# The low part of each weight: a subtraction on GpSimd and VectorE replaced by a negated copy on ScalarE and an accumulating DMA

## The chip, the cores and the metric

The kernel runs on one core of one Trainium2 chip. The metric is the device time of one execution in microseconds. A core has five engines with instruction queues of their own, which the profile calls PE (TensorE, matrix products; its weight loads are listed apart as PEld), DVE (VectorE), ACT (ScalarE), POOL (GpSimd) and SP (SyncE, which here only issues DMAs). DMAs run on 16 DMA engines that all queues share.

## The reference

The reference is one inference step of two trunk layers over 1024 prompt tokens and 64 sample tokens, all in float32:

```
h = rms_norm(x) * (1 + scale) + shift
u, v, z_a, q, k, val, z_b, g_a, g_b = split(h @ w_in)          # w_in: 1024 x 10240
y_a = gelu(u) * spatial_mix(layer_norm(gelu(v))) * silu(z_a)
y_b = combine(3 dilated window attentions of q, k, val) * silu(z_b)
merged = sigmoid(g_a) * (y_a @ w_gm_out) + sigmoid(g_b) * (y_b @ w_att_out)
x = x + gate * (merged @ w_o)
```

Outputs are the normalised result, the new keys and values, and the rows of the spatial mixer for the samples. The four weight matrices w_in, w_gm_out, w_att_out and w_o are what the change is about.

## The kernel before

**Three products in place of one.** TensorE multiplies float32r, a form of float32 with a shortened mantissa. To keep float32 precision, each operand is held as a high part (its float32r copy) and a low part (the operand minus the high part). A product of activations and weights is three matmuls: high by high, high by low, low by high. The activations are split once and stay; the weights come from HBM as raw float32 and are split on the way.

**A weight tile.** The unit is 128 x 1024 float32 (512 KB). `w_load` has SP issue the DMA of the raw tile (`wraw`); `w_split` makes `whi` with an ACT copy and `wlo` with `tensor_tensor(subtract)`, through the helper `split`, which takes the engine as `eng`: POOL on the whole tile, or for `"both"` POOL on the left half and DVE on the right half. `w_get` hands over the next tile. All raw, high and low tiles, and many others, rotate through one pool of 20 slots, so a new tile can wait for the last reader of an old one. 280 weight tiles are used, 140 for each layer.

**Main loop.** 80 of a layer's tiles are jobs on w_in. For each job `piece` runs three pieces of tokens (384, 384 and 320 columns), 24 matmuls each; between the matmuls stand those of attention and of other background work. After the matmuls of piece 0 it calls `w_ahead`, which splits the next job's tile (on POOL) and loads the one after it. The first three jobs of a layer run together, piece by piece.

**Tail.** `tail` runs nine stages for each layer (`stage_b`, `stage_a`, `stage_o`, for each of the three pieces). A weight tile serves only 24 matmuls there, so 60 tiles go by fast. After each tile's matmuls `w_ahead("both", 2)` splits up to two tiles ahead and loads a third. The last call of layer 0 already splits the first two tiles of layer 1.

**Order.** Each engine works through its instructions in the order in which the code is written; the framework adds the semaphore waits. On TensorE the first low part of a weight tile stands third among its matmuls, so a late `wlo` stops TensorE at once, and everything behind it.

Of the kernel before, what the change touches and what calls it, by code (L numbers as in the profile page):

```python
# [24 lines left out]
FT = mybir.dt.float32  # L25
FR = mybir.dt.float32r
AF = mybir.ActivationFunctionType
OP = mybir.AluOpType
# [19 lines left out]
RATE = 3.0  # L48
# [116 lines left out]
JOBS = _job_list()  # L165
# [14 lines left out]
class Builder:  # L180
# [113 lines left out]
    def w_split(self, i, eng=None):  # L294
        if i in self.wraw and i not in self.whl:
            hi = self.slot([128, 1024], FR, "whi")
            lo = self.slot([128, 1024], FR, "wlo")
            self.split(hi, lo, self.wraw.pop(i), eng or self.nc.gpsimd)
            self.whl[i] = (hi, lo)

    def w_get(self, eng=None):
# [431 lines left out]
    def piece(self, l, job, p, hi, lo, state, rate, ahead):  # L733
        nc = self.nc
        ps = self.ps("pj")
        w = PW[p]
        h = self.h[p]
        n = 0
        for k in range(8):
            for a, b in ((hi, 0), (hi, 1), (lo, 0)):  # L740
                nc.tensor.matmul(ps[:, :w], a[:, k, :], h[:, b, k, :w], start=(n == 0), stop=(n == 23))  # L741
                n += 1
            if k in (2, 5):
                self.tick(k // 3, rate)
        if ahead:
            self.w_ahead(ahead)
        self.run_later()
        getattr(self, "ev_" + job[0])(l, job, p, ps[:, :w], state)
        self.tick(2, rate)
# [641 lines left out]
    def tail(self, l, yb):  # L1391
# [31 lines left out]
        def gate_load(p, c, i, gt):  # L1423
            if c < 8:
                n = min(3, 8 - c)
                t = self.slot([128, 3, 384], name="gt")
                self.load(t[:, :n, :PW[p]], self.gs_d[l][p][:, c:c + n, i, :])
                for j in range(n):
                    gt[c + j] = t[:, j, :PW[p]]

        def stage_b(p):
            w = PW[p]
            tmp[p] = self.triple(8, name="tmp")
            gt = {}
            gate_load(p, 0, 1, gt)
            gate_load(p, 3, 1, gt)
            for i in range(4):
                ws = [t.rearrange("p (c k n) -> p c k n", c=2, n=128) for t in self.w_get()]
                for j in range(2):
                    c = 2 * i + j  # L1440
                    ps = self.ps("pj")
                    self.products(ps, w, [t[:, j] for t in ws], yb[p], 4)
                    if j == 0:
                        self.w_ahead("both", 2)
                    step()
                    nc.vector.scalar_tensor_tensor(tmp[p][c][:, :w], gt.pop(c), 1.0, ps[:, :w],
                                                   op0=OP.add, op1=OP.mult)
                    if c == 2:
                        gate_load(p, 6, 1, gt)
            del yb[p]  # L1450

        def stage_a(p):
            w = PW[p]
            m = self.act()
            mg[p] = [[m[:, e, k, :] for k in range(8)] for e in range(2)]
            gt = {}
            gate_load(p, 0, 0, gt)
            gate_load(p, 3, 0, gt)
            for c in range(8):
                ws = [t.rearrange("p (k n) -> p k n", n=128) for t in self.w_get()]  # L1460
                ps = self.ps("pj")
                self.products(ps, w, ws, ya[p], 8)
                self.w_ahead("both", 2)
                step()
                if c:
                    last()
                x = self.half(name="mx")[:, :w]
                nc.vector.scalar_tensor_tensor(x, gt.pop(c), 1.0, ps[:, :w], op0=OP.add, op1=OP.mult)
                nc.vector.tensor_tensor(x, x, tmp[p][c][:, :w], op=OP.add)
                if c == 2:  # L1470
                    gate_load(p, 6, 0, gt)
                last = lambda c=c, x=x: self.split(mg[p][0][c][:, :w], mg[p][1][c][:, :w], x)
            last()
            del ya[p], tmp[p]

        def stage_o(p):
            w = PW[p]
            wp = w if p < 2 else 256
            gate = self.mods[l]["gate"]
            x = self.triple(8, name="x")  # L1480
            self.move_x(x, self.a["xT"][:, :, P0[p]:P0[p] + w] if l == 0 else self.x_d[p], p)
            acc = self.half(name="acc")
            for c in range(8):
                ws = [t.rearrange("p (k n) -> p k n", n=128) for t in self.w_get()]
                ps = self.ps("pj")
                self.products(ps, w, ws, mg[p], 8)
                self.w_ahead("both", 2)
                step()
                if c:
                    self.sumsq(x[c - 1], c - 1, acc, p)  # L1490
                nc.vector.scalar_tensor_tensor(x[c][:, :wp], ps[:, :wp], gate[:, c, 0:1], x[c][:, :wp],
                                               op0=OP.mult, op1=OP.add)
                if wp < w:
                    t = self.half(name="xs")[:, 0:SMP]
                    nc.vector.tensor_tensor(t.rearrange("p (b t) -> p b t", t=NT),
                                            ps[:, wp:w].rearrange("p (b t) -> p b t", t=NT),
                                            gate[:, c, 1:9].unsqueeze(2).to_broadcast([128, NB, NT]), op=OP.mult)
                    nc.vector.tensor_tensor(x[c][:, wp:w], x[c][:, wp:w], t, op=OP.add)
            self.sumsq(x[7], 7, acc, p)
            del mg[p]  # L1500

            if l + 1 < L:
                self.after(lambda: self.move_x(x, self.x_d[p], p, True), 3)

            def finish():
                r = self.rstd(acc, p)
                if p < 2:
                    yield
                    yield
                    yield  # L1510
                rbc = self.rstd_bc(r, p)
                if l + 1 < L:
                    newh[p] = self.act_h(p)
                    yield from self.make_h(l + 1, p, x, rbc, newh[p])
                    return
                for c in range(8):
                    nc.vector.scalar_tensor_tensor(x[c][:, :w], x[c][:, :w], self.ng[:, L, c:c + 1], rbc[:, :w],
                                                   op0=OP.mult, op1=OP.mult)
                    self.store(a["oy"][:, c, P0[p]:P0[p] + w], x[c][:, :w])
                    yield  # L1520
            if p < 2:
                start(("h", p), finish())
            else:
                self.hgen = [iter(()), iter(()), finish()]
            if p == 2:
                if l + 1 < L:
                    self.w_load(self.wi + 3)
                    for i in range(3):
                        self.w_split(self.wi + i, "both")
# [29 lines left out]
    def run(self):  # L1559
# [5 lines left out]
        for l in range(L):  # L1565
# [11 lines left out]
            ws = [self.w_job("both") for _ in range(3)]  # L1577
            states = [{} for _ in range(3)]
            for p in range(NP):
                for _ in self.hgen[p]:  # L1580
                    pass
                for i in range(3):
                    for g in self.hgen[p + 1:p + 2]:
                        for _ in range(6):
                            next(g, None)
                    self.piece(l, JOBS[i], p, *ws[i], states[i], 0, "both" if p == 1 and i == 1 else None)
                    if p == 0 and i == 1:
                        self.w_load(self.wi + 1)
            del ws, states
            for i, job in enumerate(JOBS):  # L1590
                if i < 3:
                    continue
                if l == 0 and i == 3:
                    self.group_select()
                if job == ("ga", 1):
                    self.bgq.append(self.sample(l))
                    if l == 0:
                        self.bgq.append(self.ada(0, (4, 5)))
                    if l + 1 < L:
                        self.bgq.append(self.ada(l + 1, range(6)))  # L1600
                w, st = self.w_job(), {}
                for p in range(NP):
                    self.piece(l, job, p, *w, st, RATE / 3, self.nc.gpsimd if p == 0 else None)
                del w
                if i >= len(JOBS) - 2:
                    for _ in range(4):
                        next(pre, None)
# [102 lines left out]
```

## Time and profile before

| What | Value |
|---|---|
| median of 3 runs | 3130.92 us (3122.43 to 3131.36) |
| the profiled execution | 3131.33 us, its span 3129.5 us |
| TensorE busy | 3010.8 us, 96% of the span |
| DVE, ACT, POOL busy | 54%, 39%, 43% |
| share of the 16 DMA engines taken by the data queue | 45.4% |
| granted TensorE clock over the span | 0.98 |

The span is the time between the first and the last instruction; the other 1.8 us of the execution lie around it. Busy shares are averages over stages of different kinds: in the main loop of each layer (about 60 to 1330 us and 1620 to 2870 us) attention runs beside the projections, in the two tails (about 1370 to 1620 us and 2870 to 3129 us) little but matmuls and weight splitting is left.

### The profile page before, as it was taken

To read this page: it belongs to the slowest core of one execution; us is meant where nothing else is said; L and a number is where in the kernel's file an instruction comes from. 1 tells how busy PE (TensorE), PEld (TensorE's weight loads), DVE (VectorE), ACT (ScalarE), POOL (GpSimd) and SP (SyncE) were. 2 spreads that over 40 slices of the span, in tenths; PEclk is the share of its full clock that TensorE was granted. 3 is DMA by queue.
4 is the path that set the end of the run, shared out by engine and by line. 5 is a ranking of instruction groups with operands and counts; after the bars stand their busy time and mean duration, and the time that the engine had idled before them with its cause. 6 is when DMAs were issued, how large, how long until landed. Compare 5 with 4: busy or idle time off the path is not lost.

```text
span 3129.5 us, 51144 instructions
## 1 busy us (share of the span) xinstructions
PE 3010.8 (96%) x19136; PEld 2865.4 (92%) x19136; DVE 1687.0 (54%) x3583; ACT 1231.3 (39%) x3089; POOL 1357.9 (43%) x959
## 2 busy tenths in 40 slices
PE   6999999999998999999999999999999999999998
PEld 4999899999988998879989999999999889989998
DVE  7445546462265756466773545454513657553666
ACT  5454444444233133343444444444432331322432
POOL 4666556462143322123446755656612432222333
PEclk8999999999999999999999999999999999999999
DMA  6335353444353335466644364435343542434665
GB/s 223 113 103 119 98 101 120 95 121 84 112 180 113 122 108 167 157 236 227 211 153 134 86 142 81 119 106 114 106 81 119 171 130 95 138 102 149 223 211 172
DMA packets 262288, 425.92 MB, mean 136 GB/s; under 512 B 116140, under 2 KB 169144, under 8 KB 262040
## 3 DMA queue, kind: packets, MB, share of 16 engines
q1 hardware_dynamic: 262040, 422.65, 45.4%
q8 instruction: 151, 2.47, 0.3%
q14 instruction: 97, 0.79, 0.1%
HBM read 349.96 MB, written 72.61 MB: 135 GB/s over the span
## 4 chain that ended last, share of the span: by engine, by line
PE 82%; DVE 8%; DMA 4%; issue 3%; ACT 2%; POOL 1%; SPq 0%; DVEq 0%; ACTq 0%; POOLq 0%
PE pspj L741 53%; PE pspj L1382 14%; PE pss L870 4%; PE pso L916 3%; PE pspt L895 2%; PE psmi L602 1%; DMA kq<-in_kc_dram 1%; DVE qb L1218 1%; DMA craw<-in_wada_dram 1%; DVE chl L249 1%; PE psmi L998 1%; DMA wraw<-in_win_dram 1%; ACT whi L243 1%; PE pss L1236 1%; PE pspt L1132 1%
## 5 line engine op out<-in xcount | busy, mean ns | idle before, releaser
L741 PE MATMUL pspj<-act,whi 128*128 128x384 f32 (+1 forms) x7680 | 1967.0, 339 | 6.5 <-DVE act L674 3.5
L741 PEld LDWEIGHTS pspj<-act,whi 128*128 128x128 f32 x7680 | 1352.7, 190 | 42.4 <-issue 7.4
L741 PE MATMUL pspj<-act,wlo 128*128 128x384 f32 (+1 forms) x3840 | 1264.3, 329 | 2.3 <-POOL wlo L247 2.3
L249 POOL TENSOR_TENSOR wlo<-wraw,whi 128x1024 fp32r<-128x1024 f32 x154 | 371.4, 2411 | 970.5 <-ACT whi L243 766.5
L741 PEld LDWEIGHTS pspj<-act,wlo 128*128 128x128 f32 x3840 | 729.0, 190 | 3.4 <-POOL wlo L247 3.4
L1382 PE MATMUL pspj<-act,whi 128*128 128x384 f32 (+1 forms) x1536 | 373.4, 326 | 0.5 <-ACT act L243 0.4
L243 ACT ACTIVATE whi<-wraw 128x1024 fp32r<-128x1024 f32 x280 | 293.9, 1051 | 112.0 <-DMA wraw<-in_wgm_dram 48.1
L247 POOL TENSOR_TENSOR wlo<-wraw,whi 128x512 fp32r<-128x512 f32 x126 | 192.3, 1531 | 328.4 <-ACT whi L243 268.7
L882 ACT ACTIVATE ssb<-ssb,ast 128x128 f32<-128x128 f32 (+1 forms) x384 | 170.2, 444 | 394.2 <-DVE ast L878 394.1
L878 DVE CUSTOM_DVE_ANT_0 ssb<-pss,pack 128x128 f32<-128x128 f32 (+1 forms) x384 | 119.4, 348 | 318.1 <-PE pss L870 316.5
L1382 PEld LDWEIGHTS pspj<-act,whi 128*128 128x128 f32 x1536 | 270.0, 188 | 1.0 <-ACT act L243 0.7
L1382 PE MATMUL pspj<-act,wlo 128*128 128x384 f32 (+1 forms) x768 | 250.2, 326 | 0.0
L1010 ACT ACTIVATE th<-pspj 128x384 f32<-128x384 f32 x168 | 79.2, 471 | 428.6 <-PE pspj L741 396.5
L787 POOL TENSOR_TENSOR r<-r,sin 128x384 f32<-128x384 f32 x144 | 139.0, 965 | 141.4 <-DVE r L786 121.4
L249 DVE TENSOR_TENSOR chl<-craw,chl 128x512 fp32r<-128x512 f32 x182 | 147.2, 840 | 86.7 <-ACT chl L243 86.2
L377 POOL TENSOR_TENSOR kq<-kq,qb 128x1024 f32<-128x1024 f32 x64 | 153.5, 2404 | 63.1 <-DMA kq<-in_kc_dram 45.9
L381 POOL TENSOR_TENSOR kq<-kq,qb 128x512 f32<-128x512 f32 x128 | 167.6, 1314 | 19.8 <-DMA kq<-in_kc_dram 9.2
L386 DVE TENSOR_REDUCE sc<-kq 128x16 f32<-128x1024 f32 x128 | 155.7, 1216 | 21.2 <-POOL kq L377 20.7
L870 PE MATMUL pss<-kz,q 128*128 128x256 f32 x560 | 155.4, 385 | 10.6 <-ACT kz L240 10.6
L430 POOL TENSOR_TENSOR vq<-vq,pv 128x1024 f32<-128x1024 f32 x64 | 132.3, 2081 | 50.0 <-DMA vq<-in_vc_dram 20.6
L1382 PEld LDWEIGHTS pspj<-act,wlo 128*128 128x128 f32 x768 | 144.2, 188 | 0.0
L247 DVE TENSOR_TENSOR wlo<-wraw,whi 128x512 fp32r<-128x512 f32 x126 | 109.3, 868 | 40.0 <-ACT whi L243 36.5
(211 smaller groups left out, 3676.2 us busy)
## 6 DMA issues: line engine op xcount, KB each, us to landing
wraw<-in_win_dram SPq DMA_DIRECT2D x160, 512.0 KB
kq<-in_kc_dram SPq DMA_DIRECT2D x64, 512.0 KB
vq<-in_vc_dram SPq DMA_DIRECT2D x64, 512.0 KB
craw<-in_wada_dram SPq DMA_DIRECT2D x48, 512.0 KB
wraw<-in_wgm_dram SPq DMA_DIRECT2D x48, 512.0 KB
wraw<-in_wo_dram SPq DMA_DIRECT2D x48, 512.0 KB
kq<-in_kc_dram SPq DMA_DIRECT2D x64, 256.0 KB
craw<-in_vc_dram SPq DMA_DIRECT2D x32, 512.0 KB
```

What stands on the lines that cost most here:

```text
L243: self.nc.scalar.activation(hi, src, AF.Copy)
L247: e.tensor_tensor(lo[:, c], src[:, c], hi[:, c].bitcast(FT), op=OP.subtract)
L249: (eng or self.nc.vector).tensor_tensor(lo, src, hi.bitcast(FT), op=OP.subtract)
L377: nc.gpsimd.tensor_tensor(v, v, x, op=OP.mult)
L381: nc.gpsimd.tensor_tensor(v[:, f], v[:, 1], x[f], op=OP.mult)
L386: nc.vector.tensor_reduce(sc[:, :, i].rearrange("p h j -> p j h"), ts.pop(i)[0].rearrange("p a (j h d) -> p (a j) h d", h=2, d=64), axis=A ...
L430: nc.gpsimd.tensor_tensor(v, v, p.unsqueeze(3).to_broadcast([128, 2, 8, 64]), op=OP.mult)
L741: nc.tensor.matmul(ps[:, :w], a[:, k, :], h[:, b, k, :w], start=(n == 0), stop=(n == 23))
L787: nc.gpsimd.tensor_tensor(t2, t2, self.sin[:, s], op=OP.mult)
L870: nc.tensor.matmul(s[:, 256 * j:256 * j + 256], u["q"][:, 128 * b:128 * b + 128], self.kz[:, (b - n + j) % 4].rearrange("p h c -> p (h c)" ...
L882: nc.scalar.activation(x[:, h, :w], x[:, h, :w], AF.Exp, bias=st[:, h * 8 + b:h * 8 + b + 1], scale=-1.0, accum_out=st[:, 16 + h * 8 + b:1 ...
L1382: self.nc.tensor.matmul(ps[:, :w], ws[a][:, k, :], hs[b][k][:, :w], start=(n == 0), stop=(n == 3 * nk - 1))
```

## The change

For 274 of the 280 weight tiles `wlo` is made in another way: ACT writes `-whi` into `wlo` with a second copy of scale -1, and then POOL issues a DMA that adds the raw tile from SBUF onto `wlo` in SBUF. The other six tiles, at the start of a layer, still use `split` with `"both"`. `eng` of the calls only tells the two ways apart now.

```
         if i in self.wraw and i not in self.whl:
             hi = self.slot([128, 1024], FR, "whi")
             lo = self.slot([128, 1024], FR, "wlo")
-            self.split(hi, lo, self.wraw.pop(i), eng or self.nc.gpsimd)
+            raw = self.wraw.pop(i)
+            if eng == "both":
+                self.split(hi, lo, raw, eng)
+            else:
+                self.copy(hi, raw)
+                self.nc.scalar.activation(lo, hi.bitcast(FT), AF.Copy, scale=-1.0)
+                self.nc.gpsimd.dma_start(lo, raw, accum_op=OP.add)
             self.whl[i] = (hi, lo)
...
         if ahead:
-            self.w_ahead(ahead)
+            self.w_ahead(ahead if ahead == "both" else None)
...
-                self.w_ahead("both", 2)          # stage_b, stage_a and stage_o alike
+                self.w_ahead(None, 2)
...
-                    self.piece(l, JOBS[i], p, *ws[i], states[i], 0, "both" if p == 1 and i == 1 else None)
+                    self.piece(l, JOBS[i], p, *ws[i], states[i], 0, "both" if p == 1 and i == 1 else False)
...
-                    self.piece(l, job, p, *w, st, RATE / 3, self.nc.gpsimd if p == 0 else None)
+                    self.piece(l, job, p, *w, st, RATE / 3, p == 0)
```

ACT's queue in the tail of layer 1 (tiles 247 to 249 of the 280; `mx` is the merged activation, whose high part goes to `act`), before:

```order
L243 ACTIVATE whi_29957<-wraw_29927 128x1024
L243 ACTIVATE act_29892<-mx_29929 128x384
L243 ACTIVATE whi_29994<-wraw_29962 128x1024
L243 ACTIVATE act_29892<-mx_29966 128x384
L243 ACTIVATE whi_30036<-wraw_29999 128x1024
```

and the same tiles after, where L303 is the negated copy:

```order
L240 ACTIVATE whi_30111<-wraw_30081 128x1024
L303 ACTIVATE wlo_30112<-whi_30111 128x1024
L243 ACTIVATE act_30046<-mx_30083 128x384
L240 ACTIVATE whi_30148<-wraw_30116 128x1024
L303 ACTIVATE wlo_30149<-whi_30148 128x1024
L243 ACTIVATE act_30046<-mx_30120 128x384
L240 ACTIVATE whi_30190<-wraw_30153 128x1024
L303 ACTIVATE wlo_30191<-whi_30190 128x1024
```

ACT has one more full-tile pass behind each `whi`, ahead of the activations' own high parts; nothing else changes place on it.

POOL's queue in the main loop of layer 0 (tiles 40 to 42; `kq` are products of cached keys and queries in the background work), before:

```order
L249 TENSOR_TENSOR wlo_7661<-wraw_7472,whi_7660 128x1024
L381 TENSOR_TENSOR kq_7638<-kq_7638,qb_7516 128x512 x2
L381 TENSOR_TENSOR kq_7753<-kq_7753,qb_7516 128x512 x2
L249 TENSOR_TENSOR wlo_7835<-wraw_7664,whi_7834 128x1024
L249 TENSOR_TENSOR wlo_8022<-wraw_7838,whi_8021 128x1024
```

and after, where L304 is the accumulating DMA:

```order
L304 DMA wlo_7697<-wraw_7508 128x1024
L387 TENSOR_TENSOR kq_7674<-kq_7674,qb_7552 128x512 x2
L387 TENSOR_TENSOR kq_7790<-kq_7790,qb_7552 128x512 x2
L304 DMA wlo_7872<-wraw_7701 128x1024
L304 DMA wlo_8060<-wraw_7876 128x1024
```

Each subtraction on POOL has become the issue of a DMA in the same place of its queue. On DVE 120 half-tile subtractions have gone from the tails, and nothing stands in their place.

## Rows read from the trace of the kernel before

**Rows 1.** The page, part 1: busy time, share of the span, instructions.
```profile
PE 3010.8 (96%) x19136; PEld 2865.4 (92%) x19136; DVE 1687.0 (54%) x3583; ACT 1231.3 (39%) x3089; POOL 1357.9 (43%) x959
```

**Rows 2.** Windows by stage: length, busy us per engine, PEclk, DMA share, GB/s.
```profile
400.00:760.00 360.00, 355.97 (x2434) 341.01 (x2433) 182.25 (x457) 164.24 (x504) 201.02 (x157) 1.00 0.47 106
1370.00:1620.00 250.00, 246.93 (x1499) 245.22 (x1497) 182.33 (x283) 103.40 (x154) 99.66 (x69) 1.00 0.63 211
2870.00:3129.00 259.00, 245.48 (x1476) 243.26 (x1474) 173.01 (x281) 96.50 (x142) 92.60 (x63) 0.97 0.62 211
```

**Rows 3.** The page, part 5: groups of instructions; busy, mean ns, idle before.
```profile
L741 PE MATMUL pspj<-act,wlo 128*128 128x384 f32 (+1 forms) x3840 | 1264.3, 329 | 2.3 <-POOL wlo L247 2.3
L249 POOL TENSOR_TENSOR wlo<-wraw,whi 128x1024 fp32r<-128x1024 f32 x154 | 371.4, 2411 | 970.5 <-ACT whi L243 766.5
...
L243 ACT ACTIVATE whi<-wraw 128x1024 fp32r<-128x1024 f32 x280 | 293.9, 1051 | 112.0 <-DMA wraw<-in_wgm_dram 48.1
L247 POOL TENSOR_TENSOR wlo<-wraw,whi 128x512 fp32r<-128x512 f32 x126 | 192.3, 1531 | 328.4 <-ACT whi L243 268.7
...
L247 DVE TENSOR_TENSOR wlo<-wraw,whi 128x512 fp32r<-128x512 f32 x126 | 109.3, 868 | 40.0 <-ACT whi L243 36.5
```

**Rows 4.** Waits of PE: who waited for whom, us, times, longest.
```profile
PE pss L1228 <- DVE qb L1218: 20.3, 6, 5.3
PE pspt L1315 <- DVE chl L249: 14.8, 16, 2.8
PE pss L870 <- ACT kz L240: 10.6, 7, 3.0
...
PE psmi L639 <- POOL rstd L630: 4.4, 2, 3.4
...
PE pspj L602 <- POOL chl L249: 2.4, 4, 1.0
PE pspj L741 <- POOL wlo L247: 2.3, 3, 1.2
```

**Rows 5.** Timeline of tile 40 in the main loop: start, length, instruction.
```profile
710.83 1.06 ACT L243 ACTIVATE whi<-wraw 128x1024 fp32r<-128x1024 f32 x1
...
711.97 2.38 POOL L249 TENSOR_TENSOR wlo<-wraw,whi 128x1024 fp32r<-128x1024 f32 x1 [2.53 <-ACT whi L243]
...
722.28 0.34 PE L741 MATMUL pspj<-act,wlo 128*128 128x384 f32 x1
```

**Rows 6.** Timeline of tiles 236 and 250 in the tail.
```profile
2930.71 1.06 ACT L243 ACTIVATE whi<-wraw 128x1024 fp32r<-128x1024 f32 x1 [0.88 <-DMA wraw<-in_wo_dram]
...
2942.18 0.33 PE L1382 MATMUL pspj<-act,wlo 128*128 128x384 f32 x1
...
2995.88 1.06 ACT L243 ACTIVATE whi<-wraw 128x1024 fp32r<-128x1024 f32 x1 [4.95 <-DMA wraw<-in_wgm_dram]
...
3000.42 0.33 PE L1382 MATMUL pspj<-act,wlo 128*128 128x384 f32 x1
```

**Rows 7.** The tiles whi and wlo: duration min/median/max, first and last start.
```profile
L243 ACT ACTIVATE whi<-wraw x280: 1037/1051/1065, 52.5 to 3103.5; 128x1024 fp32r<-128x1024 f32 x140
...
L1382 PE MATMUL pspj<-act,wlo x768: 309/334/346, 1384.2 to 3115.9; 128*128 128x384 f32 x128, 128*128 128x320 f32 x64
```

**Rows 8.** Timeline at the change of layer: tile 140.
```profile
1606.76 1.04 ACT L243 ACTIVATE whi<-wraw 128x1024 fp32r<-128x1024 f32 x1
...
1609.44 0.34 PE L741 MATMUL pspj<-act,wlo 128*128 128x384 f32 x1
```

**Rows 9.** The chain that ended last: a load of a tile that it waited for.
```profile
1598.62 3.19 DMA wraw<-in_win_dram
```

**Rows 10.** Timeline in the tail: two loads issued by SP, and ACT waiting for one.
```profile
2941.85 0.81 SPq L252 DMA_DIRECT2D wraw<-in_wo_dram  x2
...
2947.51 1.06 ACT L243 ACTIVATE whi<-wraw 128x1024 fp32r<-128x1024 f32 x1 [4.54 <-DMA wraw<-in_wo_dram]
```

**Rows 11.** The window of 10 us in the tail with the fullest DMA engines.
```profile
1560.00:1570.00 10.00, 10.00 (x70) 10.00 (x69) 9.07 (x14) 4.63 (x7) 4.77 (x5) 1.00 1.01 376
```

More of the change, by code (lines that the diff above doesn't have):

```diff
@@ L1462, in stage_a @@
                 self.products(ps, w, ws, ya[p], 8)
-                self.w_ahead("both", 2)
+                self.w_ahead(None, 2)
                 step()
@@ L1486, in stage_o @@
                 self.products(ps, w, ws, mg[p], 8)
-                self.w_ahead("both", 2)
+                self.w_ahead(None, 2)
                 step()
```

## The prediction

> **What bounds the kernel now.** I read the page's busy shares first, then the windows by stage, the waits of TensorE, and last the timeline around single weight tiles. The busy shares show TensorE at work for 96% of the span and no other engine above 54% [rows 1]. The windows show where the rest lies: in both tails TensorE is busy 247 of 250 and 245 of 259 us at a granted clock of 1.00 and 0.97, and in the main loop 356 of 360 us [rows 2]. So the whole idle time of TensorE is 3129.5 - 3010.8 = 119 us, a ceiling on any gain that does not shorten the matmuls, and the change leaves the matmuls alone. The waits of TensorE show who ends its idle time: mostly DVE and ACT, in the background work and attention; the low parts of the weights account for 2.3 us in the main matmuls [rows 3, 4]. The operations that the change removes are thus hidden already. What counts is whether their replacement stays hidden.
>
> **What goes.** POOL loses 154 whole tiles x 2.411 us = 371 us and 120 halves x 1.531 = 184 us, DVE 120 halves x 0.868 = 104 us [rows 3]. All of it lies beside TensorE's matmuls. The worth is what TensorE waits for POOL: 4.4 + 2.4 + 2.3 us in the rows shown [rows 4], of which only the 2.3 are this operation; I book -4 us for that and for a little quicker POOL.
>
> **What comes on ACT.** 274 more full-tile copies x 1.051 us [rows 3] = 288 us; ACT goes from 1231 to 1519 us, 49% of the span. Each stands ahead of ACT's next evacuation or attention copy and can delay it by 1.05 us. TensorE waits 10.6 us for ACT's `kz` copies in attention [rows 4], the longest of its waits for ACT in the main loop. At best the added copies fill idle time, 0 us; at worst all 154 of the main loop lie on the path, 162 us. With ACT idle for more than half of the window 400 to 760 us [rows 2] I stand near the low end: +8 us.
>
> **What comes on the DMA engines, seen as latency.** A low part used to be ready about 2.4 us after POOL took it up. Now it is ready 1.05 us (negation) plus L after `whi`, with L = the issue on POOL plus the landing of the DMA. The trace has no DMA from POOL and none that adds, so I bound L. A plain load of the same 512 KB lands in 3.2 us where the chain waits for one [rows 9]; in a tail, of two loads issued from 2941.85 us on, the one that ACT waits for has landed at 2947.51, 5.7 us later [rows 10]. An SP issue takes about 0.4 us (half of 0.81) [rows 10]; POOL's can be as short, or as long as the subtraction it replaces, 2.4 us [rows 3]. The adding DMA must read two tiles where a copy reads one. In the fullest window of the tails the DMA engines move 376 GB/s at a share of 1.01 [rows 11], so one pass of 524,288 bytes costs 524,288 / 372,000 = 1.4 us of all sixteen. Low end, no extra pass: 3.2 + 0.4 = 3.6 us. High end, two passes one after another on top of a crowded load and a slow issue: 5.7 + 2 x 1.4 + 2.4 = 10.9 us. I take the middle of the two landings, one extra pass and a quick issue: 4.45 + 1.4 + 0.4 = about 6 us.
>
> Now the margins, from the end of a tile's `whi` to TensorE's first matmul with its `wlo`. In the main loop tile 40 has 722.28 - 711.89 = 10.4 us [rows 5]. I paired all the 280 `whi` rows (52.5 to 3103.5 us) with the first use of their low parts (in the tails the last group begins at 3112.8 us, within the rows that end at 3115.9) [rows 7]. For the main loop's changed tiles the quartiles are 9.4 to 12.3 us. With 1.05 + 6 = 7.05 us needed, nearly all of them stay covered; where POOL is still busy with `kq` products, one tile falls 1.3 us short. The exceptions are the first two tiles of layer 1, which the last stage of layer 0 splits: tile 140 has 1609.44 - 1607.80 = 1.6 us [rows 8] and 141 as little, so each is 5.4 us late. Main loop: 12 us. In the tails a tile lasts one group of 24 matmuls and the margins are shorter, 7.1 us in the middle: 2942.18 - 2931.77 = 10.4 for tile 236, but 3000.42 - 2996.94 = 3.5 for tile 250, whose `whi` had waited for its raw tile [rows 6]. Of the 120 tail tiles 58 have less than 7.05 us, and the shortfalls sum to 65 us in the first tail and 41 in the second: 106 us. For L = 3.6 the same count gives 6 us in the main loop and 19 in the tails; for 10.9 it gives 205 and 565. These are shortfalls against the old schedule. A stop of TensorE gives later tiles time, but it also keeps slots and raw tiles longer; I leave the two against each other.
>
> **The same, seen as throughput.** The tails use the DMA engines for 0.63 x 250 = 158 and 0.62 x 259 = 161 us already [rows 2]. Sixty adding DMAs each at one pass (1.4 us) add 84 us: 242 and 245, which just fits. At two passes 168 us: 326 and 329 us of work in 250 and 259, so +76 and +70 if packed perfectly. At three, +160 and +154. The share counts time in which packets wait for HBM, which these transfers between SBUF tiles do not touch, so two passes are dearer here than they should be: I put this route at two thirds, about +100. Both routes meet near 100; they are one delay seen twice and are not added.
>
> Beside it: the Trainium skill, "Collectives: The Full Stack", section on the fold count, says that a reducing DMA is slower since the add needs two source reads on one ring, and halves the rate. By that it is two passes, the estimate above; no row of before shows it. "DMA: Bandwidth & Descriptors", section on the anatomy of a DMA from GpSimd, gives 2.0 us + bytes / 436e3 per us, an estimate of 3.2 us for 512 KB; by that the hidden case below holds. The row of 3.2 us for a plain load agrees with its size, and the two rules part over the second read.
>
> **Sum.** 3131.3 (the profiled execution; span 3129.5 + 1.8 around it; it lies 0.4 us above the median, so no shift) + 106 (tails) + 12 (main loop and change of layer) + 8 (ACT) - 4 (POOL) = 3253, say 3250 us.
>
> **Rivals.**
> 1. *The adder is slow.* Three passes or more, L near 11 us: the tails are bound by the DMA engines, +314 by throughput, and the main loop's 10.4 us margin is broken, +205: 3131 + 314 + 205 = 3650 us. For: nothing in the trace shows an adding DMA at a copy's speed. Against: at a share of 0.47 in the main loop [rows 2] there is room.
> 2. *The transfer is hidden.* L about 3.6 us, one pass: 3131 + 6 + 19 + 8 - 4 = 3160, and if the stops give back half of what they take, 3145 us. For: the margins of 10 us, and a share of 0.63 leaves room. Against: a raw tile in the tails lands after 5.7 us already.
> 3. *Faster: the relief counts.* If L stays under 3.6 us and POOL and DVE, freed of 659 us, deliver the background work sooner, the waits for DVE `qb` and `chl` and for POOL in [rows 4] could shrink: 20.3 + 14.8 + 4.4 + 2.4 + 2.3 = 44 us, of which perhaps a third goes: 3116 us. It decides from the point where no low part is late. Against: DVE is relieved in the tails, while those waits stand in the background work of the main loop.
> 4. *POOL is not relieved*, since making the DMA's descriptors costs it as much as the subtraction: L grows by 2 us to 8, the shortfalls to 256 in the tails and 35 in the main loop: 3430 us.
>
> **How the numbers follow.** Forecast 0.50; rival 1 0.17; rival 2 0.18; rival 3 0.06; rival 4 0.09. The forecast's own range is 3180 to 3350 (L from 4.5 to 7.5 us). A measurement here tells 0.3%, some 9 us, from no change. Faster by more: rival 3, 0.06. Within: the lower half of rival 2, 0.08. Slower: the rest, 0.86. The range of 8 in 10 runs from 3135, which leaves out rival 3 and a part of rival 2, to 3600, which leaves out most of rival 1.
>
> **What would show it.** The page of the changed kernel has a queue of its own for POOL's DMAs; its share over 274 DMAs gives the passes (one pass: 274 x 1.4 / 3250 = 12% of the engines; two: 24%). The chain gains pieces of DMA `wlo<-wraw` in the tails and hardly any in the main loop. TensorE's idle time before `wlo` matmuls rises from 2.3 to some 100 us, most of it in the two tail windows, which grow by some 50 us each. ACT's busy time rises by 288 us without new waits of TensorE for ACT. I am wrong if the tails keep their length (rival 2 or 3), or if the main loop's windows grow by as much as the tails (rival 1).

## The result and the profile after

| | before | after |
|---|---|---|
| median, same chip | 3129.0 us (4 runs) | 3381.2 us (3368.1 to 3384.2, 4 runs) |
| ratio to before | | 1.080 [1.077, 1.084] |
| span of the profiled execution | 3129.5 us | 3366.4 us |
| granted TensorE clock over the span | 0.98 | 0.96 |

The changed kernel is 252 us slower. The forecast was 3250 us, 121 us more than this median of before: the sign held, and the time lies in the range of 8 in 10 (3135 to 3600), but above the forecast's own range of 3180 to 3350, and the loss is twice as large. The two profiled executions lie 236.9 us apart; that difference is what is explained below.

First the page: the busy shares (part 1, with share of the span and instructions), which answer to [rows 1], and the DMA queues (part 3: packets, MB, share of 16 engines).

```profile
PE 3086.8 (92%) x19136; PEld 2921.7 (87%) x19136; DVE 1499.2 (45%) x3463; ACT 1517.3 (45%) x3363; POOL 1045.0 (31%) x959
...
q1 hardware_dynamic: 262040, 422.65, 41.4%
q0 software_dynamic: 39456, 143.67, 22.9%
```

TensorE runs the same 19136 matmuls, yet they take 3086.8 - 3010.8 = 76.0 us longer. Its idle time went from 118.7 to 3366.4 - 3086.8 = 279.6 us, up by 160.9. The two make 236.9 us, the whole difference. POOL and DVE are relieved as planned, and it buys nothing. The new queue q0 holds the 274 adding DMAs: 0.229 x 3366.4 / 274 = 2.81 us of all sixteen engines for each, twice the 1.4 us of one pass [rows 11].

Next the windows by stage (length, busy us of PE, PEld, DVE, ACT, POOL, then PEclk, DMA share, GB/s), which answer to [rows 2]; the second and third are the two tails.

```profile
400.00:760.00 360.00, 347.51 (x2331) 330.72 (x2329) 174.44 (x457) 181.89 (x513) 170.01 (x157) 0.99 0.56 132
1408.00:1730.00 322.00, 266.39 (x1463) 258.45 (x1462) 111.23 (x219) 166.60 (x214) 62.33 (x70) 0.92 0.98 265
3028.00:3360.00 332.00, 270.93 (x1474) 261.47 (x1472) 104.39 (x216) 158.38 (x201) 54.51 (x63) 0.91 0.94 254
```

In the tails the DMA share went from 0.63 and 0.62 to 0.98 and 0.94 over a longer stretch, and TensorE's granted clock fell from 1.00 and 0.97 to 0.92 and 0.91. In the main loop the share is 0.56, and 2331 matmuls were done where 2434 were before.

For the lengths by stage I cut each trace at the first matmul with a weight tile of a stage (main loop 0 begins with the span, tail 1 ends with it):

| us | main loop 0 | tail 0 | main loop 1 | tail 1 |
|---|---|---|---|---|
| before | 1367.1 | 242.0 | 1260.6 | 259.8 |
| after | 1406.7 | 322.5 | 1298.3 | 339.0 |
| difference | +39.6 | +80.5 | +37.7 | +79.2 |

A main loop that an edit leaves as it is moves by some 10 us to either side (main loop 0 with its subtraction came out at 1356.6 to 1372.4 us below, beside 1367.1 here), so a single difference of 10 us tells nothing there; a tail with its subtraction moves by 3 us at most (241.7 to 243.9, 258.8 to 261.7).

The groups (busy, mean ns | idle just before, what ended most of it) answer to [rows 3]:

```profile
L747 PE MATMUL pspj<-act,wlo 128*128 128x384 f32 (+1 forms) x3840 | 1271.3, 331 | 36.7 <-DMA wlo<-wraw 35.6
L304 POOL DMA_DIRECT2D wlo<-wraw x274 | 240.6, 878 | 1727.7 <-ACT wlo L303 1132.9
...
L1388 PE MATMUL pspj<-act,wlo 128*128 128x384 f32 (+1 forms) x768 | 269.3, 351 | 77.7 <-DMA wlo<-wraw 77.5
```

and the waits of TensorE (us, times, longest) to [rows 4]:

```profile
PE pspj L1388 <- DMA wlo<-wraw: 110.4, 45, 8.3
PE pspj L747 <- DMA wlo<-wraw: 35.6, 18, 5.7
PE pspt L1321 <- DVE chl L249: 18.6, 12, 4.1
PE pss L1234 <- DVE qb L1224: 15.9, 6, 4.1
PE pss L1105 <- DVE vn L1119: 15.3, 4, 4.3
```

L747 is the main loop's matmul, L1388 the tails' (L741 and L1382 before). Of the 161 us more idle, 110.4 + 35.6 = 146.0 stand in front of a low part. The old waits for DVE are about what they were; the one for `vn`, an intermediate of the spatial mixer, is new.

`vn` neither reads nor writes a weight, but it takes a slot of the pool of 20. The group that writes it, before and then after, with what ended the idle time before it:

```profile
L1113 DVE TENSOR_SCALAR vn<-pss,mv 128x512 f32<-128x512 f32 (+1 forms) x36 | 27.4, 802 | 4.3 <-POOL wlo L249 3.0 <-POOL mv L1106 1.3
```

```profile
L1119 DVE TENSOR_SCALAR vn<-pss,mv 128x512 f32<-128x512 f32 (+1 forms) x36 | 27.4, 803 | 22.0 <-issue 10.8 <-DMA wlo<-wraw 9.8 <-POOL mv L1112 1.4
```

In the trace the `vn` behind each of the four waits starts within 0.2 us after an adding DMA has landed, the two put down to "issue" too: its slot is held by the adding DMA, where the subtraction gave it back sooner. The issues of loads by SP meet the same, before and then after:

```profile
SPq L252 <- POOL wlo L249: 111.6, 26, 14.0
```

```profile
SPq L252 <- DMA wlo<-wraw: 323.8, 65, 14.0
```

How one low part comes late in a tail, in the timeline (start, length, instruction [idle before <- what ended it]), to be held against [rows 6]:

```profile
1498.53 1.05 ACT L240 ACTIVATE whi<-wraw 128x1024 fp32r<-128x1024 f32 x1
...
1499.61 1.06 ACT L303 ACTIVATE wlo<-whi 128x1024 fp32r<-128x1024 f32 x1
...
1501.07 0.88 POOL L304 DMA_DIRECT2D wlo<-wraw  x1 [10.94 <-ACT wlo L303]
...
1509.68 0.69 PE L1388 MATMUL pspj<-act,wlo 128*128 128x384 f32 x1 [7.69 <-DMA wlo<-wraw]
```

`whi` is done at 1499.58, the negation at 1500.67, POOL begins to issue 0.4 us later and takes 0.88 us, and TensorE gets the low part at 1509.68, 8.6 us after the issue began, having stood still for 7.69 us. The windows around that moment show why:

```profile
1490.00:1500.00 10.00, 9.95 (x58) 9.63 (x57) 4.16 (x8) 3.63 (x7) 0.14 (x1) 1.00 1.05 323
1500.00:1510.00 10.00, 2.31 (x13) 1.99 (x12) 1.18 (x2) 6.46 (x8) 2.61 (x3) 0.79 1.06 340
1510.00:1515.00 5.00, 5.00 (x23) 5.00 (x23) 0.00 (x0) 1.62 (x3) 0.89 (x1) 0.74 1.07 212
```

The DMA engines are full before, during and after the stop, and the granted clock, 1.00 before TensorE stood still, averages 0.74 when it works again. Main loop, tile 23, answers to [rows 5]; SPq rows are SP's DMA issues:

```profile
439.46 1.04 ACT L240 ACTIVATE whi<-wraw 128x1024 fp32r<-128x1024 f32 x1
...
441.94 0.41 SPq L252 DMA_DIRECT2D kq<-in_kc_dram  x1
442.01 0.90 POOL L304 DMA_DIRECT2D wlo<-wraw  x1 [3.87 <-ACT wlo L303]
443.23 0.56 SPq L252 DMA_DIRECT2D kq<-in_kc_dram  x1
443.85 1.40 SPq L252 DMA_DIRECT2D wraw<-in_win_dram  x1
...
452.47 0.69 PE L747 MATMUL pspj<-act,wlo 128*128 128x384 f32 x1 [3.76 <-DMA wlo<-wraw]
```

Three loads of SP were issued within 2 us of the addition, and the low part took 10.4 us from its issue. The DMA engines were full meanwhile (first window below, share 1.01). TensorE stood still for 3.76 us, and in the 5 us of the second window its granted clock was 0.51 (the lower of its two levels, 1.2 GHz):

```profile
443.00:453.00 10.00, 6.24 (x39) 5.87 (x38) 0.51 (x4) 1.93 (x8) 1.11 (x1) 0.90 1.01 237
453.00:458.00 5.00, 5.00 (x17) 4.82 (x16) 0.51 (x4) 0.88 (x4) 1.24 (x1) 0.51 0.64 264
```

The landing of the adding DMAs, from the view of the tile `wlo` in 60 to 1330 us (main loop) and then in 1408 to 1730 us (tail):

```profile
DMA to landing us min/median/max: 4.5/4.9/13.0
```

```profile
DMA to landing us min/median/max: 4.5/7.5/10.7
```

Of the 154 adding DMAs of the two main loops, ten take more than 10 us. During each of these the data queue's own packets take 6 to 12 us of all sixteen engines; where SP issues nothing from 4 us before the addition to 3 us after it, the median landing is 4.6 us.

Last, a piece of the chain of waits in the second tail (start, us, what), which stands for about five like it:

```profile
3243.74 6.11 DMA wraw<-in_wo_dram
3249.93 1.07 ACT whi L240
3251.02 1.06 ACT wlo L303
...
3252.49 7.56 DMA wlo<-wraw
3260.09 5.51 PE pspj L1388 x21
```

In 22 us of the end's history TensorE has 5.5; the load and the addition, both on the DMA engines, have 13.7.

### The profile page after: what moved, and what is told of

Same layout as the page of the kernel before. It is cut to its first block, busy times and chain, and to the rows that moved or that the text cites. A ratio compares the mean times of both kernels' runs of the same rounds, so it can differ in the third digit from the quotient of the medians.

```text
span 3366.4 us, 51449 instructions
## 1 busy us (share of the span) xinstructions
PE 3086.8 (92%) x19136; PEld 2921.7 (87%) x19136; DVE 1499.2 (45%) x3463; ACT 1517.3 (45%) x3363; POOL 1045.0 (31%) x959
## 3 DMA queue, kind: packets, MB, share of 16 engines
q0 software_dynamic: 39456, 143.67, 22.9%
## 5 line engine op out<-in xcount | busy, mean ns | idle before, releaser
L747 PE MATMUL pspj<-act,whi 128*128 128x384 f32 (+1 forms) x7680 | 1975.3, 340 | 5.2 <-DVE act L680 3.2
L747 PEld LDWEIGHTS pspj<-act,whi 128*128 128x128 f32 x7680 | 1359.4, 191 | 41.4 <-issue 7.6
L747 PE MATMUL pspj<-act,wlo 128*128 128x384 f32 (+1 forms) x3840 | 1271.3, 331 | 36.7 <-DMA wlo<-wraw 35.6
L304 POOL DMA_DIRECT2D wlo<-wraw x274 | 240.6, 878 | 1727.7 <-ACT wlo L303 1132.9
L747 PEld LDWEIGHTS pspj<-act,wlo 128*128 128x128 f32 x3840 | 732.8, 191 | 43.6 <-DMA wlo<-wraw 42.0
L1388 PE MATMUL pspj<-act,whi 128*128 128x384 f32 (+1 forms) x1536 | 399.4, 345 | 0.3
L1388 PE MATMUL pspj<-act,wlo 128*128 128x384 f32 (+1 forms) x768 | 269.3, 351 | 77.7 <-DMA wlo<-wraw 77.5
L303 ACT ACTIVATE wlo<-whi 128x1024 fp32r<-128x1024 f32 x274 | 290.5, 1060 | 23.4 <-DVE lng L1127 4.8
L1388 PEld LDWEIGHTS pspj<-act,whi 128*128 128x128 f32 x1536 | 293.2, 203 | 1.1 <-DVE act L249 1.1
L1016 ACT ACTIVATE th<-pspj 128x384 f32<-128x384 f32 x168 | 79.2, 471 | 386.2 <-PE pspj L747 382.7
L1388 PEld LDWEIGHTS pspj<-act,wlo 128*128 128x128 f32 x768 | 155.9, 203 | 88.5 <-DMA wlo<-wraw 88.2
L793 POOL TENSOR_TENSOR r<-r,sin 128x384 f32<-128x384 f32 x144 | 146.2, 1015 | 166.7 <-DVE r L792 148.8
L243 ACT ACTIVATE chl<-craw 128x512 fp32r<-128x512 f32 x192 | 113.2, 622 | 56.1 <-DMA craw<-in_vc_dram 29.6
```

The costliest lines, as they stand in the source:

```text
L303: self.nc.scalar.activation(lo, hi.bitcast(FT), AF.Copy, scale=-1.0)
L304: self.nc.gpsimd.dma_start(lo, raw, accum_op=OP.add)
L793: nc.gpsimd.tensor_tensor(t2, t2, self.sin[:, s], op=OP.mult)
L1388: self.nc.tensor.matmul(ps[:, :w], ws[a][:, k, :], hs[b][k][:, :w], start=(n == 0), stop=(n == 3 * nk - 1))
```

## The experiments

All kernels were timed against before on the same chip, where before took 3120.4 us (e1 to e4), 3129.0 (e5 to e8) and 3128.0 (e10, e11); the stage lengths come from one profiled execution of each, cut as above, and are held against the one profile of before.

| us | ratio to before | main 0 | tail 0 | main 1 | tail 1 |
|---|---|---|---|---|---|
| after | 1.080 [1.077, 1.084] | 1406.7 | 322.5 | 1298.3 | 339.0 |
| e1: tails as before | 1.029 [1.026, 1.032] | 1409.7 | 241.7 | 1298.1 | 259.7 |
| e2: main loop as before | 1.051 [1.049, 1.054] | 1356.6 | 331.3 | 1252.1 | 332.3 |
| e3: negation, addition on engines | 1.015 [1.013, 1.017] | 1375.2 | 252.7 | 1272.1 | 263.9 |
| e4: low part last | 1.059 [1.056, 1.062] | 1393.5 | 305.3 | 1275.9 | 328.0 |
| e5: before, low part last | 1.000 [0.998, 1.001] | 1372.4 | 243.6 | 1256.6 | 261.7 |
| e6: plain copy for the addition | 1.040 [1.038, 1.042] | 1395.4 | 278.1 | 1288.8 | 297.8 |
| e7: before, idle DMAs in the tails | 1.033 [1.031, 1.036] | 1366.3 | 294.1 | 1262.8 | 311.9 |
| e8: half the addition in the tails | 1.055 [1.052, 1.058] | 1411.8 | 274.4 | 1298.5 | 296.1 |
| e10: e1, low part last | 1.015 [1.013, 1.018] | 1396.6 | 243.9 | 1287.9 | 258.8 |
| e11: before, idle DMAs in the main loop | 1.025 [1.023, 1.028] | 1410.9 | 242.6 | 1292.4 | 259.8 |

**e1 and e2: which stage.** e1 is after with the tails' `w_ahead(None, 2)` put back to `"both"`; e2 gives the main loop its subtraction again:

```
+            elif i % 140 < 81 and i != 140 and i != 141:
+                self.split(hi, lo, raw, self.nc.gpsimd)
```

> The tails make their low parts as before (subtraction in halves on POOL and DVE), the main loop keeps the accumulating DMA. Theory A (a low part lands too late, TensorE stops, and after each stop the granted clock is 0.5 for some microseconds, so that a stop costs its length and then some): the tails lose nothing, the main loop its 77 us: 3205 us, TensorE at a clock of 0.5 for about 160 us (122 before, 265 with the change in both). Theory B (the DMA engines are full, which holds up every load): they were full in the tails alone, so the main loop loses little: 3140 to 3160 us. Theory C (the second pass on ACT delays what stands behind it): the main loop has 152 of the 274 passes, so about 55% of the 252 us stay: 3270 us.

> The main loop makes its low parts as before (subtraction on POOL), the tails keep the accumulating DMA. Theory A: the tails lose 160 us: 3290 us. Theory B: nearly all of the loss is here: 3350 us. Theory C: 122 of 274 passes, 45% of 252: 3240 us.

Measured: 3208.7 and 3279.6 us. The main loop's part alone costs 2.9%, the tails' part alone 5.1%; together 8.0, as the whole. So the two add, and the numbers of theory A came out in both: the tails lose two thirds, and the main loop, which the prediction had at 12 + 8 us, loses a third, 88 us in e1. They tell theory A from B and C as stated, but any cause that acts within its own stage would give them, so why each stage loses is left to the runs below.

**e3: without the DMA.** ACT negates, and POOL and DVE add the raw weights:

```
-                self.nc.gpsimd.dma_start(lo, raw, accum_op=OP.add)
+                if i % 140 < 81 and i != 140 and i != 141:
+                    self.nc.gpsimd.tensor_tensor(lo, raw, lo.bitcast(FT), op=OP.add)
+                else:
+                    for e, c in ((self.nc.gpsimd, slice(512)), (self.nc.vector, slice(512, None))):
+                        e.tensor_tensor(lo[:, c], raw[:, c], lo[:, c].bitcast(FT), op=OP.add)
```

> ACT makes the negated copy as in the change, but POOL (in the tails POOL and DVE in halves) adds the raw tile onto it; there is no accumulating DMA. Theories A and B: the loss goes, but for the 1.05 us that each low part is later: 3125 to 3150 us. Theory C: the loss stays: 3300 us or more.

Measured: 3167.4 us, 1.5% slower: far below theory C, and some 17 us above the upper end of A and B. ACT's second pass, which stands ahead of every low part, is not free: about 47 us by the medians, 34 of it in the profiled execution, spread over all four stages (+8, +11, +11, +4; the main loops' are about what an unchanged one moves by). The rest, 6.5%, comes with the DMA.

**e4 and e5: late or slow.** The eight products with the weight's low part stand last of the 24, so that it has some 2.5 us more (in the main loop the first of them starts 2.9 us into a group, in place of 0.35, by the medians); e4 does this to after, e5 to before, in `piece` as in the tails' `products`, which is shown:

```
-            for a, b in ((0, 0), (0, 1), (1, 0)):
-                self.nc.tensor.matmul(ps[:, :w], ws[a][:, k, :], hs[b][k][:, :w], ...)
+        for a, b, k in [(0, b, k) for k in range(nk) for b in range(2)] + [(1, 0, k) for k in range(nk)]:
+            self.nc.tensor.matmul(ps[:, :w], ws[a][:, k, :], hs[b][k][:, :w], ...)
```

> The change, with the 24 matmuls of a group in another order: the 16 with the weight's high part first, the 8 with its low part last. The first use of a low part comes some 14 matmuls later, 14 x 0.174 = 2.4 us. Theory A: with 2.4 us more margin the shortfalls in the tails shrink from 170 to about 45 us and in the main loop to under 10, and most of the low clock goes with them: 3180 to 3220 us. Theory B: the DMA engines have as much to move in the tails, so these stay near their length: 3340 us or more. Theory C: 3340 us or more, as ACT has the same work.

> The kernel before, with only the order of the 24 matmuls changed (the weight's low part last). Both theories: TensorE waits 2.3 us for low parts there, so at most some us are to be had: 3110 to 3125 us beside 3120 of before.

Measured: e4 3305.0 us, between the theories; e5 3126.0 us, the same as before, so the order by itself is worth nothing. In e4 the main loops win back 13 and 22 us, the tails only 17 and 11 of their 80, and the stops before low parts there go from 110.4 to 88.6 us, no further. Its tail windows show what holds them:

```profile
1420.00:1690.00 270.00, 227.53 (x1276) 219.68 (x1274) 95.33 (x186) 147.06 (x189) 53.98 (x61) 0.95 1.01 274
3000.00:3290.00 290.00, 249.81 (x1387) 240.57 (x1385) 95.05 (x195) 146.55 (x186) 50.05 (x57) 0.94 0.99 269
```

At a DMA share of 1.01 and 0.99 more time for one tile only moves the wait.

**e6: one pass in place of two.** The DMA copies the raw weights where it added them; the addition is left out, so this kernel computes something else.

```
-                self.nc.gpsimd.dma_start(lo, raw, accum_op=OP.add)
+                self.nc.gpsimd.dma_start(lo, raw)
```

> The change with the DMA from POOL copying the raw tile instead of adding it: one read in place of two, all else alike, so the low parts hold the raw weights (the addition is left out). Theory A (the tails lose time since low parts land too late): the landing gets about 1.3 us shorter, shortfalls in the tails fall from 166 to about 70 us, the half clock comes on top: 3270 us. Theory B (the tails are bound by the time of the DMA engines: 158 us of other traffic and 60 x 2.6 us of adding DMAs, 315 us in a stage of 242; only the main loop loses by lateness): at 1.3 us per DMA 158 + 76 = 234 us fit, so the tails come back to within some 15 us each, and the main loop keeps some 40 us: 3190 us.

Measured: 3253.0 us, nearer theory A; the tails keep 36 and 38 us, where theory B gave some 15 each. The queue, the tails' windows, and the landing in the view of the tile:

```profile
q0 software_dynamic: 39456, 143.67, 13.3%
```

```profile
1400.00:1670.00 270.00, 242.27 (x1425) 235.81 (x1424) 105.93 (x209) 161.14 (x209) 39.59 (x67) 0.99 0.90 308
2960.00:3230.00 270.00, 238.08 (x1366) 232.09 (x1366) 93.74 (x187) 151.34 (x191) 31.77 (x58) 0.96 0.87 299
```

```profile
DMA to landing us min/median/max: 2.8/4.2/15.5
```

A copy takes 0.133 x 3260.1 / 274 = 1.58 us of the sixteen engines against the addition's 2.81, and at best 2.8 us to land against 4.5. With as many issues on POOL (0.56 us each in place of 0.88) and the same pass on ACT, what adding costs over copying is half of the loss: 4.0% in place of 8.0. The Trainium skill, "Collectives: The Full Stack", section on the fold count, puts the reducing step of a ring collective at half the rate of a copy, because the add needs two source reads; the two queue rows agree, at 1.78 times.

**e7: about the same traffic, no matmul waiting for it.** Before, with two DMAs from POOL for each of 118 tail tiles that write its `whi` to device memory, where nothing reads it:

```
+            if i % 140 >= 81:
+                for r in range(2):
+                    self.nc.gpsimd.dma_start(self.idle_d[...], hi.bitcast(FT))
```

> The kernel before, with two extra DMAs for each of 118 tail tiles, issued from POOL, that write the high part to scratch memory in HBM; no instruction reads what they write. They give the DMA engines of each tail as much more work as the adding DMAs did. Theory A: no low part is later, so the time stays within 15 us of before: 3120 to 3135 us. Theory B: 158 + 59 x 2 x 1.3 = 311 us of DMA work in tails of 242 and 259 us: 3230 to 3250 us.

Measured: 3236.6 us, theory B. Two idle DMAs take 2 x 0.096 x 3235.0 / 236 = 2.63 us of the sixteen engines, an addition 2.81. The tails grow by 52 us each with no low part behind a DMA, at a full DMA share:

```profile
1370.00:1670.00 300.00, 262.99 (x1493) 254.64 (x1491) 193.23 (x278) 102.23 (x152) 162.50 (x185) 0.95 0.98 380
2930.00:3220.00 290.00, 254.73 (x1426) 247.35 (x1425) 177.67 (x261) 95.48 (x137) 156.41 (x176) 0.93 1.01 389
```

Over the tails as cut, of 294.1 and 311.9 us, all packets take 294 and 303 us of the sixteen engines. The engines' time thus makes some 52 of the 80 us of a tail: raw tiles come late, and with them high and low parts (21.5 and 18.6 us of waits for `whi` and `wlo`) and DVE's `tmp`, which in its three longest waits stands behind a late load, of a raw tile or of `gt` (24.1 us, 2.0 before):

```profile
PE pspj L1386 <- DVE tmp L1450: 24.1, 9, 5.5
PE pspj L1386 <- ACT whi L243: 21.5, 9, 5.7
PE pspj L1386 <- POOL wlo L247: 18.6, 17, 1.4
```

One thing does wait for the idle DMAs: they hold the slot of `whi`, and SP's issues of loads waited for them 42 times, 134.0 us in all. With the engines full, a share of 0.98 and 1.01, an earlier issue had little to win; that is argued, not tested.

**e8: half the DMA work in the tails.** There ACT negates and the DMA adds only the left half; DVE subtracts the right half.

```
+                m = 512 if i % 140 >= 81 or i in (140, 141) else 1024
+                self.nc.scalar.activation(lo[:, :m], hi[:, :m].bitcast(FT), AF.Copy, scale=-1.0)
+                self.nc.gpsimd.dma_start(lo[:, :m], raw[:, :m], accum_op=OP.add)
+                if m < 1024:
+                    self.nc.vector.tensor_tensor(lo[:, m:], raw[:, m:], hi[:, m:].bitcast(FT), op=OP.subtract)
```

> The change, but in the tails the negation and the adding DMA take the left half of a tile, and DVE subtracts the right half. Theory A: half a tile lands at most 1.3 us sooner, so the tails keep about half of their loss of 160 us: 3280 us. Theory B: 158 + 60 x 1.3 = 236 us fit into 242: the tails lose some 15 us each, the main loop its 77: 3225 us.

Measured: 3297.3 us, nearer theory A. The tails keep +32 and +36 us of 80, though the work nearly fits: all packets take 251 and 254 us of the sixteen engines, where the tails of before are 242.0 and 259.8 us long. At this level the wait for the single low part rules:

```profile
1415.00:1680.00 265.00, 240.60 (x1414) 234.62 (x1413) 140.53 (x268) 136.34 (x208) 59.60 (x67) 0.99 0.92 255
```

```profile
PE pspj L1391 <- DMA wlo<-wraw: 50.3, 30, 6.4
```

**e10 and e11: why the main loop loses.** e10 is e1 with the order of e4. e11 is before with e7's two idle DMAs, here for 156 tiles of the main loop (`if 3 <= i % 140 < 81`); here SP waits for none of them.

> The change in the main loop alone (tails as before), and in all weight matmuls the products with the low part of the weight stand last of the 24, so that each low part has some 5 us more. The change in the main loop alone cost 88 us over before (3208.7 against 3120.4). Theory A (most of that is low parts that are late because the adding DMA shares the DMA engines with background loads, and the half clock behind each such stop of TensorE): TensorE's idle time before wlo falls below 8 us for both main loops together, the main loops to some 1390 and 1275 us, total 3150 to 3175 us. Rival B (the loss is ACT's second pass and the DMA engines' share, which slow the background work whether or not a low part is late): total 3195 to 3210 us, as without the new order.

> The kernel before, with two DMAs from POOL for each of 156 main-loop tiles that write its high part to device memory, where nobody reads it: the DMA work of the addition and POOL's issues in the main loop, with no instruction that waits for them and no second pass on ACT. Theory A (the main loop loses by low parts that are late, and by ACT; the DMA engines have room there): within 10 us of before, 3120 to 3140 us. Rival B (the added DMA work delays the background loads and TensorE waits for those): 30 to 60 us slower, 3155 to 3185 us.

Measured: e10 3178.0 us (+50 over before, where e1 had +88) and e11 3207.8 us (+80). TensorE's waits for low parts, in e1 and then in e10:

```profile
PE pspj L747 <- DMA wlo<-wraw: 37.0, 18, 4.4
```

```profile
PE pspj L746 <- DMA wlo<-wraw: 9.7, 6, 5.0
```

With them the loss fell by 38 us (88 - 50, by the medians; 23 by the profiled main loops); about 50 stay, most of which are not late low parts. The new order gives 2.5 us, as in e4, not the 5 that were expected. By its total e10 falls just outside theory A, by its main loops (1396.6 and 1287.9 us) between A and B. e11 refutes theory A outright and goes beyond B: idle traffic in the main loop, where the share over 400 to 760 us is 0.59, costs as much as the change. Its waits, which stood at 14.8 and 20.3 us [rows 4] and 4.8 us before:

```profile
PE pspt L1319 <- DVE chl L249: 24.9, 12, 4.8
PE pss L1232 <- DVE qb L1222: 24.3, 6, 6.5
PE pso L1330 <- DVE oh L1326: 16.0, 10, 3.2
```

They belong to the background work, which is fed by loads; no low part is late there. Two reservations: e11 writes to device memory where the addition stays in SBUF, and its POOL issues come on top of the subtractions. So its 80 us are what such traffic can do, not a share of the 88.

Where the main loop's 77 us (profiled; 88 by the medians of e1) lie can be read from the two traces, cut by stage. TensorE is idle for 54 us more in the two main loops: 34 in front of low parts, 15 behind `vn`, which waits for a slot, and some 4 elsewhere. Its matmuls take 24 us longer. Of the causes, late low parts are worth 23 to 38 us (e1 less e10), with the clock behind them; the wait for `vn` stays at 17.0 us in e10; ACT's pass costs up to some 20 (e3), in part by making the low parts later. These overlap and are not to be added. What later loads cost beyond that, which e11 shows to be possible, no run measured for the traffic inside SBUF itself; that share stays open.

## Why the prediction was right in sign and off by half

The terms of the sum beside what the two profiled executions give:

| us | forecast | measured | from |
|---|---|---|---|
| stops before low parts, tails | 106 | 110.4 | waits of L1388 |
| stops before low parts, main loop and change of layer | 12 | 35.6 | waits of L747 |
| all other idle time of TensorE | 8 - 4 | 14.9 | 160.9 - 146.0 |
| the same matmuls lasting longer | 0 | 76.0 | PE busy |
| sum | 122 | 236.9 | spans |

By stages the sum is short by 54 us in the tails (106 forecast, 80.5 + 79.2 = 160 measured) and by 61 us in the main loops with the change of layer (12 + 8 - 4 = 16 forecast, 77 measured).

**What held.** TensorE was the bound and the removed subtractions were hidden: POOL lost 313 us of busy time and TensorE gained nothing. POOL's issue, put at 0.4 us, takes 0.88 us, well below the 2.4 us of rival 4, which falls. The two passes are there: q0 at 22.9%, where 24% was named. ACT's busy time rose by 286 us (288 forecast). Rival 1 falls, since the main loop grew by half as much as the tails and the adder takes two passes; rival 2 falls with the second pass and a landing of 4.5 us at best, rival 3 with the sign.

**What came out by luck.** The stops before low parts in the tails are 110 us for 106. But L, put at 6 us, is 7.5 us in the median there (6.5 over all 274), and for that the prediction's own count of margins gives some 210 us (it has 256 for 8 us). The stops stayed at half of that. The likely reason is that a stop gives the tiles behind it time, which the prediction named and left out of the count; no run tests it.

**The failed step: the throughput of the tails, cut to two thirds.** The prediction had 326 and 329 us of DMA work for the tails at two passes, +76 and +70, and discounted it to "about +100", because the old share might be waiting for HBM. No row shows such a discount: the data queue took 0.454 x 3129.5 = 1421 us of the sixteen engines before and 0.414 x 3366.4 = 1394 after, and q0's 771 came on top. The tails are 322.5 and 339.0 us long at shares of 0.98 and 0.94: the uncut figure was right to 10 us. e7 and e4 show that it is the bound: the traffic lengthens the tails with no matmul waiting for it, and more time for each low part does not shorten them by more than 17 us. The agreement of the two routes near 100, taken as support, was made by the discount. Uncut they disagreed, 146 against 106, and a sum of stops is not the length of a stage: stops are only the part of the loss in which TensorE stands still.

**The missing term: the clock behind each stop.** The margins count idle time, and the sum took the matmuls as fixed. In the trace the granted clock stood at its lower level for 263 us, where it was 121 before, and the matmuls took 76 us longer. The stop at 452 us shows it: 3.76 us of rest, then 0.51 for 5 us. In the tails, 107 us more idle time and 53 us of longer matmuls make up the 160: with the clock added, the route by stops meets the uncut throughput. Since the DMA engines set the length there, this slowness partly covers waiting that would have been there anyway (argued from the full share; no run separates the two). In the main loops, where the lower level lasted 41 us longer than before, the other 24 of the 76 us are loss. The Trainium skill, "TensorE: Matmul & The Clock Gate", section Terms, puts the penalty at the throttled time by the part of the clock withheld; by that an estimate of 143 x 0.5 = 72 us, and the 76 of the two profiles agree.

**The mis-sized term: the main loop.** One L of 6 us against margins of 9.4 to 12.3 (10.4 to 12.3 when counted again) left nearly all tiles covered. Of the 12 us, 10.8 were for tiles 140 and 141 at the change of layer, and there TensorE stood still for 1.1 us. The other 34.5 us of stops fell on tiles that the prediction had covered but for 1.3 us: L is 4.9 us in the median of layer 0, but over 10 us for those that meet a burst of loads, and six stops of 3.8 to 5.7 us, all behind such a landing, make 25 us of it. A second term was put at nothing: the prediction named the slots and raw tiles that are kept longer and left them against the time that stops give back; `vn` waited for such slots, which cost TensorE 15.3 us. ACT's pass, put at 8, costs up to some 20 (e3). "At a share of 0.47 there is room", said of rival 1, was an average over bursts.

**Would a part of it pay?** No. The main loop alone loses 2.9%, 1.5% with the low part last; the tails 5.1%; the negated copy without a DMA 1.5%. None beats the kernel before, and e5, its reordering, equals it.

## What to carry to other kernels

To move work to the DMA engines, add its passes to each stage's DMA time as it stands (an adding DMA of SBUF tiles counts nearly twice a copy); where the sum exceeds the stage's length, take the sum as the new length and do not discount it. Below that, judge lateness by the landing in bursts, not by the median, and by the loads of others that the traffic delays: a share of 0.5 is no proof of room. When the bounding engine is TensorE, price a stop at its length plus the half-clock stretch behind it, here about 0.5 us for each 1 us of added idle time (76 to 161; 0.3 to 0.8 in the other slower runs). And count how long a DMA that reads a tile holds its slot: here until it had landed, for everyone who shares the pool.

## What was not expected of the hardware

Relieving POOL shortened operations on DVE that the change does not touch. DVE's busy time fell by 188 us, of which only 103 are the removed halves. The row of an untouched subtraction in the tails, in the view of the tile `prep` (count: min/median/max ns), before and then after:

```profile
L249 DVE TENSOR_TENSOR act<-prep,act x48: 477/551/1652, 1374.4 to 3020.6; 128x384 fp32r<-128x384 f32 x32, 128x320 fp32r<-128x320 f32 x16
```

```profile
L249 DVE TENSOR_TENSOR act<-prep,act x48: 484/552/560, 1413.2 to 3220.8; 128x384 fp32r<-128x384 f32 x32, 128x320 fp32r<-128x320 f32 x16
```

The median is the same; the longest, 1652 ns, is gone with POOL's 1531 ns half subtractions [rows 3]. Of the 48 before, 15 took more than 1 us, and each of them overlapped a half subtraction on POOL. So DVE's operation had been stretched while POOL worked, and the profile books that as busy. The Trainium skill, "SBUF — State Buffer", section on the two separate sides, says that a DVE operation with two SBUF inputs and a GpSimd one that reads SBUF hold a port pair in turn, each for the whole instruction; these rows agree. It gained no time here, since DVE was not what TensorE waited for in the tails.
